# Value columns of a projection in two double blocks: products of 512 columns instead of 256

## The chip, the cores and the metric

The kernel runs on one core of a Trainium2 chip. The metric is the device time of one execution in microseconds, the median of several runs. The core's engines are TensorE (matmuls, PE in the profile, PEld its weight loads), VectorE (DVE), ScalarE (ACT), GpSimd (POOL) and SyncE (SP); 16 DMA engines move data.

## The reference, cut to what matters

One block of a network: a normalized input `xn` (256 tokens, 2048 wide) and a normalized context `cn` (256 tokens) are multiplied by a wide matrix `w_in`, and the columns of the product feed a windowed attention and two gated scans.

```
aq, ak, av, ag, hq, hff, hfb, hi, hg, ma, mb = split_columns(xn @ w_in[l])
caq, cak, cav, cag, chq, chff, chfb, chi, chg, cma, cmb = split_columns(cn @ w_in[l])
...
v_h = to_heads(hi)
cv_h = to_heads(chi)
```

The change touches the columns `hi` and `chi` alone: the 2048 values (from column 11264, `C_HI`) of the scans, for the 256 tokens and the 256 of the context. All is float32.

## The kernel before

`xH` and `xL` (one tile, `xHL`) hold the 512 normalized rows, transposed and split in a high and a low part, so that one float32 product is three matmuls: high by high, low by high and high by low. Weights arrive as raw tiles of 128x1024 (`wload`, 5 buffers, one load of 512 KB on SP's queue). ScalarE rounds a raw tile to its high part `wh`, and VectorE subtracts it to get the low part `wl` (`two`, three buffers each). I call the work of one such pair a chunk.

The stage of the change computes five groups of columns after the output gates: values (4 calls of `quad_tok`), keys and values of the attention (2 calls), and then the forget gates (`quad_col`). They use a scheme with seven products instead of eight for a 2x2 block product: the tokens are halved (latent and context halves side by side), the 2048 rows of K are halved, and the columns of a block are halved. `token_sums` has put sums of token parts in `S`; `combos` makes the combinations of the weight blocks b11, b12, b21, b22 on VectorE; `ORDER` lists the seven products, each with its weight combination and its token operand (a part of `xHL` or of `S`).

`quad_tok(col0, dst)` does 512 columns in two column halves of 256. It loops over two halves `s` of the K rows of a block. In each it loads four raw tiles (one for each weight block, 4 row tiles by 256 columns), and for each of the seven products makes one chunk and issues 24 matmuls of 256 moving columns: 16 with `wh` (L732, L734) and 8 with `wl` (L737). A product has its own bank of the accumulating memory (tiles `pj` and `pm`) through both halves of K. After the second half `done_with` adds the banks up: ScalarE copies out two, and VectorE makes seven additions of 512 columns. Two stores of 512 KB on POOL's queue put the result in `v_dr`. In one call there are 2 x 7 chunks and 336 matmuls; four calls give 56 chunks and 1344 matmuls.

The names in the instructions: `T` is a buffer for a weight combination (two of them, in turn), `vo` a result, `sn` a sum on the way, `sgg` and `hg` belong to the output gates. `tc.high_priority` moves an instruction forward in the order that the scheduler writes for VectorE and ScalarE; TensorE's order is the code's order. Each queue runs its instructions in order.

Of the kernel before, what the change touches and what calls it, by code (L numbers as in the profile page):

```python
# [7 lines left out]
F32 = mybir.dt.float32  # L8
F32R = mybir.dt.float32r
U8 = mybir.dt.uint8  # L10
AF = mybir.ActivationFunctionType
ALU = mybir.AluOpType
PSUM = bass.MemoryType.PSUM

P = 128
# [6 lines left out]
PRIO = 100000  # L22

C_Q, C_K, C_V, C_G = 0, 2048, 2560, 3072
C_HQ, C_FF, C_FB, C_HI, C_HG = 5120, 7168, 9216, 11264, 13312
# [13 lines left out]
def block_kernel(ctx: ExitStack, tc: tile.TileContext, x, c, cx, c_ctx, w_ada, b_ada, norm_gain, w_in,  # L39
                 b_merge, lb_f, lb_b, hg_gain, w_oh, sink, w_oa, w_out, fin_gain, cst, msk, out):  # L40
    nc = tc.nc
    pe, act, dve, pool = nc.tensor, nc.scalar, nc.vector, nc.gpsimd

    def pl(name, bufs=1, **kw):
        return tc.tile_pool(name=name, bufs=bufs, **kw)
# [3 lines left out]
    fp = ctx.enter_context(pl("fp", side="right"))  # L49
    pad = ctx.enter_context(pl("pad"))  # L50
    base = ctx.enter_context(pl("base"))
# [9 lines left out]
    def wload(w, row0, nk, col0, ncol, rp=None):  # L61

        raw = (rp or wp).tile([P, 1024], F32, tag="raw", name="raw", bufs=8 if rp else 5)
        rv = raw[:, : len(col0) * nk * ncol].rearrange("p (g k c) -> p g k c", g=len(col0), k=nk)
        for g, co in enumerate(col0):
            nc.sync.dma_start(rv[:, g], w[row0: row0 + nk * P, co: co + ncol].rearrange("(k p) c -> p k c", p=P))
        return raw, rv
# [37 lines left out]
    def bank(name="pj"):  # L105
        return pj.tile([P, 512], F32, tag="pj", name=name)
# [122 lines left out]
    v_dr = [[dram.tile([P, 1024], F32, name=f"v{g}_{t}") for t in range(2)] for g in range(4)]  # L229
# [275 lines left out]
    def bank8():  # L505

        i = turn8[0] % 8
        turn8[0] += 1
        return bank() if i < 4 else ps.tile([P, 512], F32, tag=("tp", "o", "al1", "al2")[i - 4], name="pm")
# [5 lines left out]
    def pairs_of(a):  # L515
        return a.rearrange("p (a t) -> p a t", a=2)

    def run(g):
        for _ in g:
            pass  # L520
# [3 lines left out]
    def send():  # L524
        while outs:
            o = outs.pop(0)
            nc.scalar.dma_start(*o[:2])
            tasks.extend(o[2:])

    def output_gate(g):  # L530
        bg = yield from proj_tok_g(w_in, C_HG + 512 * g, x_st, range(2))
        for t in range(2):
            sg = base.tile([P, 512], F32, tag="sm", name="sgg", bufs=3)
            act.activation(sg, bg[t], AF.Sigmoid)
            dve.tensor_tensor(sg, bg[t], sg, op=ALU.mult)
            outs.append((hg_dr[g][:, t * 512: (t + 1) * 512], sg))
# [24 lines left out]
    with pl("sp", reuse_waits="tile") as sp:  # L561
# [3 lines left out]
        def tmp():  # L565
            t_at[0] ^= 1
            return sp.tile([P, 1024], F32, tag="T", name="T") if t_at[0] else \
                fp.tile([P, 1024], F32, tag="acc", name="T")
# [33 lines left out]
        def sums(i):  # L602
            return lambda k: S[:, :, i, k, :].rearrange("p z (a t) -> p z a t", a=2)

        def sides(h, kh):
            return lambda k: xHL[:, :, 8 * kh + k, :].rearrange("p z (a h t) -> p z a h t", a=2, h=2)[:, :, :, h, :]

        ORDER = ((0, "b11", sides(0, 0)), (1, "t1", sums(0)), (2, "t2", sums(1)), (3, "b22", sums(3)),
                 (4, "t3", sums(2)), (5, "b21", sides(0, 1)), (6, "t4", sides(1, 1)))

        def combos(b):


            def sub(o, x_, y_):
                with tc.high_priority(PRIO):
                    dve.tensor_tensor(o, x_, y_, op=ALU.subtract)  # L616

            t = tmp()
            yield b["11"]
            sub(t, b["12"], b["11"])  # L620
            yield t
            sub(t, b["22"], t)
            yield t
            yield b["22"]
            sub(b["12"], b["22"], b["12"])
            yield b["12"]
            yield b["21"]
            sub(t, b["21"], t)
            yield t

        def two(src):
            h = wp.tile([P, 1024], F32R, tag="wh", name="wh", bufs=3)
            lo = wp.tile([P, 1024], F32R, tag="wl", name="wl", bufs=3)
            with tc.high_priority(PRIO):
                act.activation(h, src, AF.Copy)  # L635
                dve.tensor_tensor(lo, src, h.bitcast(F32), op=ALU.subtract)  # L636
            return h, lo
# [49 lines left out]
        def quad_tok(col0, dst):  # L687

            m_ = [None] * 7
            out = [fp.tile([P, 2, 512], F32, tag="F0", name="vo", bufs=2) for _ in range(2)]  # L690
            sn = {}

            def add(o, x_, y_):
                dve.tensor_tensor(o, x_, y_, op=ALU.add)

            def done_with(i):


                def place(t, c):
                    return out[t][:, :, c * T: (c + 1) * T]  # L700

                with tc.high_priority(2 * PRIO):
                    if i < 2:
                        sn[i] = base.tile([P, 512], F32, tag="sm", name="sn", bufs=3)
                        act.activation(sn[i], m_[i], AF.Copy)
                    elif i == 2:
                        sn[2] = base.tile([P, 512], F32, tag="bb", name="sn", bufs=2)
                        add(sn[2], m_[2], sn[0])
                    elif i == 3:
                        sn[3] = base.tile([P, 512], F32, tag="bb", name="sn", bufs=2)  # L710
                        add(sn[3], sn[2], sn[1])
                        add(place(0, 1), pairs_of(m_[3]), pairs_of(sn[3]))
                    elif i == 4:
                        add(sn[2], m_[4], sn[2])
                        add(place(1, 1), pairs_of(sn[2]), pairs_of(sn[1]))
                    elif i == 5:
                        add(place(0, 0), pairs_of(m_[5]), pairs_of(sn[0]))
                    else:
                        add(place(1, 0), pairs_of(m_[6]), pairs_of(sn[2]))

            for s in range(2):
                b = {n: wload(w_in, 1024 * (n[0] == "2") + 512 * s, 4, (col0 + T * (n[1] == "2"),), T)[0]
                     for n in ("11", "12", "22", "21")}
                for (i, _, st_), src in zip(ORDER, combos(b)):
                    h, lo = [a.rearrange("p (k c) -> p k c", k=4) for a in two(src)]
                    if s == 0:
                        m_[i] = bank8()
                    st4 = [(k, z) for k in range(4) for z in range(2)]
                    for k, z in st4:
                        o = m_[i][:, z * T: (z + 1) * T]  # L730
                        sh, sl = [st_(4 * s + k)[:, a, z, :] for a in range(2)]
                        pe.matmul(o, sh, h[:, k, :], start=s == 0 and k == 0 and z == 0, stop=False,  # L732
                                  skip_group_check=True)
                        pe.matmul(o, sl, h[:, k, :], start=False, stop=False, skip_group_check=True)  # L734
                    for k, z in st4:
                        o = m_[i][:, z * T: (z + 1) * T]
                        pe.matmul(o, st_(4 * s + k)[:, 0, z, :], lo[:, k, :], start=False,  # L737
                                  stop=s == 1 and k == 3 and z == 1, skip_group_check=True)
                    if s == 1:
                        done_with(i)  # L740
            for t in range(2):
                nc.gpsimd.dma_start(dst[t], out[t].rearrange("p a c -> p (a c)"))

        with tc.manual_schedule(engines={mybir.EngineType.PE}):
            for g in range(3):
                run(output_gate(g))
                send()
                if g < 2:
                    token_sums(g)
            for g in range(4):  # L750
                quad_tok(C_HI + 512 * g, v_dr[g])
            for i, co in enumerate((C_K, C_V)):
                quad_tok(co, kv_dr[i])
            for n in range(1, 8):
                for d in range(2):
                    if (d, n) != (0, 1):
                        quad_col(d, 2 * n)
# [702 lines left out]
    for n in range(3):  # L1460
        bo = [bank() for _ in range(2)]
        for k0 in range(0, KT, 2):
            h, lo = wchunk(w_out, k0 * P, 2, n * 512, 512)
# [8 lines left out]
    for k0 in range(0, KT, 4):  # L1472
        h, lo = wchunk(w_out, k0 * P, 4, D - 512, 256)
# [8 lines left out]
    for t in range(2):  # L1482
# [12 lines left out]
        for c0, c1, on_act in ((0, 512, True), (512, 1024, False), (1024, 1536, True), (1536, D, False)):  # L1495
            o_ = xv[t][:, c0: c1]
# [62 lines left out]
```

## Time and profile before

| | |
|---|---|
| median of 3 runs | 1584.49 us (1583.45 to 1588.19) |
| the profiled execution | 1586.59 us, its span 1584.8 us |
| granted TensorE clock, mean | 0.999 |
| output gates, last chunk begins | 195.5 us |
| values (4 calls of `quad_tok`) | 198.2 to 359.5 us |
| K and V of the attention (2 calls) | 359.5 to 440.1 us |
| forget gates | 440.1 to about 700 us |

Times in the profile are from the start of the span. A row that groups instructions has their count, busy time, mean length in ns, and, behind the bar, the idle time of the engine just ahead of them and what ended it. A matmul's length overlaps that of the next, so the pace of TensorE is read from the distance between starts.

### The profile page before, as it was taken

The numbers are of one execution on the slowest core, as the hardware profiler recorded it, in microseconds if no ns is written. First come the engines' busy times: TensorE is split into PE (matmuls) and PEld (weight loads), VectorE is DVE, ScalarE is ACT, GpSimd is POOL, SyncE is SP. The second block draws the span as 40 slices with busy tenths as digits, with TensorE's granted clock in tenths as the row PEclk, the third lists the DMA queues.
The fourth block names the chain that finished last, engine by engine and source line by source line (L and its number), as shares of the span: only waits on it lengthen the run. The fifth ranks groups of instructions, "written<-read, shape, count | busy, mean of one in ns | idle before, by whom it ended". The sixth has DMA issues, their size and how long they took to land. (4 is left out here: it accounts for less than half of the span.)

```text
span 1584.8 us, 27868 instructions
## 1 busy us (share of the span) xinstructions
PE 1561.6 (99%) x10954; PEld 1343.8 (85%) x10954; DVE 1201.5 (76%) x1764; ACT 860.5 (54%) x1344; POOL 142.1 (9%) x280
## 2 busy tenths in 40 slices
PE   7999999999999999999999999999999999999998
PEld 4568899999988888888888888888888888888887
DVE  4449977777787878878888897888878777757764
ACT  4336443333355555566656666575666776744442
POOL 2000000000000000011212222121121000000000
PEclk9999999999999999999999999999999999999999
DMA  9996734434444444467777877878677854458661
GB/s 366 386 387 230 226 111 130 134 132 134 133 147 127 134 130 137 136 225 252 243 247 244 300 260 233 270 243 273 221 261 249 289 159 154 155 180 295 226 197 69
DMA packets 242900, 333.83 MB, mean 211 GB/s; under 512 B 12080, under 2 KB 162000, under 8 KB 242000
## 3 DMA queue, kind: packets, MB, share of 16 engines
q1 hardware_dynamic: 214096, 249.54, 48.5%
q0 software_dynamic: 19168, 64.08, 11.8%
q10 hardware_dynamic: 9504, 18.42, 3.2%
q8 instruction: 86, 1.41, 0.4%
q14 instruction: 46, 0.38, 0.1%
HBM read 300.53 MB, written 31.47 MB: 209 GB/s over the span
## 5 line engine op out<-in xcount | busy, mean ns | idle before, releaser
L85 ACT ACTIVATE wh<-raw 128x1024 fp32r<-128x1024 f32 x284 | 298.8, 1059 | 236.3 <-PE pj L101 151.7
L86 DVE TENSOR_TENSOR wl<-raw,wh 128x1024 fp32r<-128x1024 f32 x284 | 344.0, 1219 | 89.9 <-ACT wh L85 88.9
L100 PE MATMUL pj<-wh,xHL 128*128 128x512 f32 (+1 forms) x768 | 298.6, 390 | 0.0
L101 PE MATMUL pj<-wh,xHL 128*128 128x512 f32 (+1 forms) x768 | 294.8, 385 | 0.0
L103 PE MATMUL pj<-wl,xHL 128*128 128x512 f32 (+1 forms) x768 | 202.7, 385 | 0.0
L635 ACT ACTIVATE wh<-T 128x1024 fp32r<-128x1024 f32 x75 | 79.5, 1060 | 166.8 <-DVE T L616 83.9
L100 PEld LDWEIGHTS pj<-wh,xHL 128*128 128x128 f32 x768 | 144.4, 188 | 28.2 <-ACT sg L219 0.6
L101 PEld LDWEIGHTS pj<-wh,xHL 128*128 128x128 f32 x768 | 144.5, 188 | 27.6
L103 PEld LDWEIGHTS pj<-wl,xHL 128*128 128x128 f32 x768 | 142.0, 188 | 28.9
L635 ACT ACTIVATE wh<-raw 128x1024 fp32r<-128x1024 f32 x100 | 105.3, 1055 | 71.9 <-PE pj L734 23.7
L154 PE MATMUL pj<-xHL,wh 128*128 128x512 f32 x512 | 130.3, 396 | 0.0
L636 DVE TENSOR_TENSOR wl<-raw,wh 128x1024 fp32r<-128x1024 f32 x100 | 121.8, 1218 | 9.8 <-ACT wh L635 9.7
L636 DVE TENSOR_TENSOR wl<-T,wh 128x1024 fp32r<-128x1024 f32 x75 | 91.5, 1220 | 32.8 <-ACT wh L635 32.8
L154 PEld LDWEIGHTS pj<-xHL,wh 128*128 128x128 f32 x512 | 92.4, 189 | 16.9
L157 PEld LDWEIGHTS pj<-xHL,wl 128*128 128x128 f32 x512 | 69.8, 190 | 5.2
L204 DVE SCALAR_TENSOR_TENSOR acc<-hgw,cg,acc 128x512 f32<-128x512 f32 x60 | 44.9, 748 | 35.0 <-DMA hgw<-in_w_ada_dram 35.0
L157 PE MATMUL pj<-xHL,wl 128*128 128x256 f32 x512 | 71.3, 282 | 0.0
L912 DVE TENSOR_TENSOR A<-A,X 128x512 f32<-128x512 f32 x96 | 61.6, 682 | 0.1
L616 DVE TENSOR_TENSOR T<-raw,T 128x1024 f32<-128x1024 f32 x50 | 60.9, 1218 | 0.1
L616 DVE TENSOR_TENSOR raw<-raw 128x1024 f32<-128x1024 f32 x25 | 30.6, 1225 | 36.7 <-DMA raw<-in_w_in_dram 36.7
L541 POOL DMA_DIRECT2D hgw<-in_w_ada_dram x64 | 35.0, 547 | 235.3 <-DVE acc L204 157.6
L660 PE MATMUL pj<-S,wh 128*128 128x512 f32 x208 | 52.6, 395 | 1.6 <-ACT s L667 1.6
(353 smaller groups left out, 3155.1 us busy)
## 6 DMA issues: line engine op xcount, KB each, us to landing
raw<-in_w_in_dram SPq DMA_DIRECT2D x300, 512.0 KB, 4.6
raw<-in_w_ada_dram SPq DMA_DIRECT2D x64, 512.0 KB, 8.0
hgw<-in_w_ada_dram POOLq DMA_DIRECT2D x64, 256.0 KB, 4.5
raw<-in_w_o_hgrn_dram SPq DMA_DIRECT2D x32, 512.0 KB, 3.6
raw<-in_w_o_attn_dram SPq DMA_DIRECT2D x32, 512.0 KB, 4.1
raw<-in_w_out_dram SPq DMA_DIRECT2D x28, 512.0 KB, 4.1
F<-F POOLq DMA_DIRECT2D x16, 512.0 KB, 7.2
F<-F ACTq DMA_DIRECT2D x13, 512.0 KB, 4.4
```

Source lines behind the costliest of these rows:

```text
L85: last_hi[0] = act.activation(h[:, :n], raw[:, :n], AF.Copy).ins
L86: last_lo[0] = dve.tensor_tensor(lo[:, :n], raw[:, :n], h[:, :n].bitcast(F32), op=ALU.subtract).ins
L100: pe.matmul(o, s[0], m[0], start=first, stop=False)
L101: pe.matmul(o, s[1], m[0], start=False, stop=False)
L103: pe.matmul(o, s[0], m[1], start=False, stop=last)
L154: pe.matmul(o.rearrange("p (a t) -> p a t", a=2), h[:, j, cs_], xHL[:, :, k0 + j, :T], start=k0 + j == 0, stop=False)
L157: pe.matmul(o[:, :T], lo[:, j, cs_], xH[:, k0 + j, :T], start=False, stop=k0 + j == KT - 1)
L616: dve.tensor_tensor(o, x_, y_, op=ALU.subtract)
L635: act.activation(h, src, AF.Copy)
L636: dve.tensor_tensor(lo, src, h.bitcast(F32), op=ALU.subtract)
L660: pe.matmul(m_[z].rearrange("p (z a t) -> p z a t", z=2, a=2), h[:, k, :], mv(k), start=fresh and k == 0, stop=False, skip_group_check=True)
L912: dve.tensor_tensor(av, av, f.unsqueeze(3).to_broadcast([P, 2, n2, b]), op=ALU.mult)
```

## The change

Two calls of a new function, `quad_wide(b)`, take the place of the four calls of `quad_tok` for the values. The attention's K and V and the forget gates stay as they are.

- One call does 1024 columns in two column halves of 512. A raw tile is now 2 row tiles by 512 columns, and a chunk is 12 matmuls of 512 moving columns: 8 with `wh`, 4 with `wl`. Each weight block needs two raw tiles, so that each product is two chunks and a half of K needs 8 raw tiles and 14 chunks. Two calls give again 56 chunks, with 672 matmuls.
- Both `T` buffers together hold one weight combination.
- A product fills two banks, one for each half of the tokens. There are three pairs of banks for each half of K, not seven banks for a call: products 0, 2, 4 and 6 are accumulated in pair 0, products 1 and 3 in pair 1, product 5 has pair 2. What pair 0 and pair 1 hold after products 0, 1 and 2 is copied out by ScalarE (`kept`, in the buffers F0 and F1), and VectorE adds it to a bank after products 3, 4 and 5.
- Each half of K stores its result on its own, in 3 stores of 512 KB and 2 of 256 KB on POOL's queue. The second half's stores add to what stands in memory (`accum_op`), so that the two halves of K meet there.

```
def quad_wide(b):
    def less(o, x_, y_):
        with tc.high_priority(PRIO):
            for o_, a_, b_ in zip(o, x_, y_):
                dve.tensor_tensor(o_, a_, b_, op=ALU.subtract)
    def weights(s):
        def load(n):
            return [wload(w_in, 1024 * (n[0] == "2") + 512 * s + 256 * c, 2,
                          (C_HI + 1024 * b + 512 * (n[1] == "2"),), 512)[0] for c in range(2)]
        u = [tmp(), tmp()]
        b11 = load("11")
        yield b11
        b12 = load("12")
        less(u, b12, b11)
        yield u
        b22 = load("22")
        less(u, b22, u)
        yield u
        yield b22
        less(b12, b22, b12)
        yield b12
        b21 = load("21")
        yield b21
        less(u, b21, u)
        yield u
    for s in range(2):
        m_ = [[bank8(), bank8()] for _ in range(3)]
        into = {0: (0, True), 1: (1, True), 2: (0, False), 3: (1, False), 4: (0, False), 5: (2, True),
                6: (0, False)}
        kept = {}
        def store(o, t, c, z=slice(0, 2)):
            kw = {"accum_op": ALU.add} if s else {}
            nc.gpsimd.dma_start(v_dr[2 * b + c][t].rearrange("p (z c) -> p z c", z=2)[:, z, :], o, **kw)
        def done_with(i, m):
            with tc.high_priority(2 * PRIO):
                if i < 3:
                    kept[i] = fp.tile([P, 2, 512], F32, tag="F1" if i == 2 else "F0", name="part",
                                      bufs=1 if i == 2 else 2)
                    for z in range(2):
                        act.activation(kept[i][:, z, :], m[z], AF.Copy)
                elif i < 6:
                    o = kept[5 - i]
                    for z in range(2):
                        dve.tensor_tensor(o[:, z, :], m[z], o[:, z, :], op=ALU.add)
                    store(o, *((0, 1), (1, 1), (0, 0))[i - 3])
                else:
                    for z in range(2):
                        o = base.tile([P, 512], F32, tag="bb", name="part", bufs=2)
                        act.activation(o, m[z], AF.Copy)
                        store(o, 1, 0, z)
        for (i, _, st_), tiles in zip(ORDER, weights(s)):
            z_, fresh = into[i]
            for c in range(2):
                h, lo = [a.rearrange("p (k c) -> p k c", k=2) for a in two(tiles[c])]
                jz = [(j, z) for j in range(2) for z in range(2)]
                for j, z in jz:
                    for a in range(2):
                        pe.matmul(m_[z_][z], st_(4 * s + 2 * c + j)[:, a, z, :], h[:, j, :],
                                  start=fresh and c == 0 and j == 0 and a == 0, stop=False,
                                  skip_group_check=True)
                for j, z in jz:
                    pe.matmul(m_[z_][z], st_(4 * s + 2 * c + j)[:, 0, z, :], lo[:, j, :], start=False,
                              stop=c == 1 and j == 1, skip_group_check=True)
            done_with(i, m_[z_])
...
-            for g in range(4):
-                quad_tok(C_HI + 512 * g, v_dr[g])
+            for b in range(2):
+                quad_wide(b)
```

The order of instructions is the same on every engine outside this stage. Inside it, VectorE's order before, at the end of the first call of `quad_tok` (`wl_2178` is the last chunk's low part, `wl_2220` that of the next call's first, `T_2218` and `T_2434` combinations for the next call and half):

```order
L636 TENSOR_TENSOR wl_2178<-T_1992,wh_2177 128x1024
L694 TENSOR_TENSOR vo_1766<-pj_1870,sn_2113 128x2x256
L694 TENSOR_TENSOR sn_2083<-pm_1900,sn_2083 128x512
L636 TENSOR_TENSOR wl_2220<-raw_2210,wh_2219 128x1024
L694 TENSOR_TENSOR vo_1767<-sn_2083,sn_2052 128x2x256
L694 TENSOR_TENSOR vo_1766<-pm_1929,sn_2021 128x2x256
L636 TENSOR_TENSOR wl_2250<-T_2218,wh_2249 128x1024
L616 TENSOR_TENSOR T_2434<-raw_2428,raw_2426 128x1024
L616 TENSOR_TENSOR T_2218<-raw_2214,T_2218 128x1024
L694 TENSOR_TENSOR vo_1767<-pm_1959,sn_2083 128x2x256
L636 TENSOR_TENSOR wl_2280<-T_2218,wh_2279 128x1024
```

A combination is made one product ahead, and for the next half already, in the other buffer. VectorE's order now, at the end of the first half of K of the first `quad_wide` (L750 is `less`, L796 an addition of `done_with`; `raw_2054` and `raw_2056` are b11 of the next half, `raw_2093` and `raw_2095` its b12, `raw_2134` and `raw_2136` its b22; `wl_2025` is the last chunk of this half, `wl_2059`, `wl_2075`, `wl_2100` and `wl_2116` are chunks 0 to 3 of the next; `part_1810` is what is kept of product 0):

```order
L750 TENSOR_TENSOR T_2052<-raw_2093,raw_2054 128x1024
L636 TENSOR_TENSOR wl_2025<-T_1773,wh_2024 128x1024
L750 TENSOR_TENSOR raw_2093<-raw_2134,raw_2093 128x1024
L750 TENSOR_TENSOR T_2053<-raw_2095,raw_2056 128x1024
L796 TENSOR_TENSOR part_1810<-pm_1770,part_1810 128x512
L796 TENSOR_TENSOR part_1810<-pm_1771,part_1810 128x512
L636 TENSOR_TENSOR wl_2059<-raw_2054,wh_2058 128x1024
L636 TENSOR_TENSOR wl_2075<-raw_2056,wh_2074 128x1024
L636 TENSOR_TENSOR wl_2100<-T_2052,wh_2099 128x1024
L750 TENSOR_TENSOR T_2052<-raw_2134,T_2052 128x1024
L750 TENSOR_TENSOR raw_2095<-raw_2136,raw_2095 128x1024
L636 TENSOR_TENSOR wl_2116<-T_2053,wh_2115 128x1024
```

Four subtractions for the next half stand among the splits of chunks -1 to 3; `raw_2136` goes into the buffer that `raw_2054` leaves. POOL's order before, for all of the values:

```order
L742 DMA v0_0_107<-vo_1766 128x1024
L742 DMA v0_1_108<-vo_1767 128x1024
L742 DMA v1_0_109<-vo_2208 128x1024
L742 DMA v1_1_110<-vo_2209 128x1024
L742 DMA v2_0_111<-vo_2650 128x1024
L742 DMA v2_1_112<-vo_2651 128x1024
L742 DMA v3_0_113<-vo_3092 128x1024
L742 DMA v3_1_114<-vo_3093 128x1024
```

These are two stores for each call. Now, for the first of two calls (the first five rows are the first half of K, the last five add to the same tiles in memory):

```order
L783 DMA v1_0_109<-part_1892 128x1024
L783 DMA v1_1_110<-part_1851 128x1024
L783 DMA v0_0_107<-part_1810 128x1024
L783 DMA v0_1_108<-part_2040 128x512
L783 DMA v0_1_108<-part_2043 128x512
L783 DMA v1_0_109<-part_2172 128x1024
L783 DMA v1_1_110<-part_2131 128x1024
L783 DMA v0_0_107<-part_2090 128x1024
L783 DMA v0_1_108<-part_2320 128x512
L783 DMA v0_1_108<-part_2323 128x512
```

Ten stores for each call stand where four stood for the same columns.

More of the change, by code (lines that the diff above doesn't have):

```diff
@@ L742, in quad_tok @@
                 nc.gpsimd.dma_start(dst[t], out[t].rearrange("p a c -> p (a c)"))
+        def quad_wide(b):
+            def less(o, x_, y_):
+                with tc.high_priority(PRIO):
+                    for o_, a_, b_ in zip(o, x_, y_):
[20 more added lines that the diff above has]
+                yield u
+            for s in range(2):
+                m_ = [[bank8(), bank8()] for _ in range(3)]
[6 more added lines that the diff above has]
+                def done_with(i, m):
+                    with tc.high_priority(2 * PRIO):
+                        if i < 3:
+                            kept[i] = fp.tile([P, 2, 512], F32, tag="F1" if i == 2 else "F0", name="part",
+                                              bufs=1 if i == 2 else 2)
+                            for z in range(2):
+                                act.activation(kept[i][:, z, :], m[z], AF.Copy)
+                        elif i < 6:
+                            o = kept[5 - i]
+                            for z in range(2):
+                                dve.tensor_tensor(o[:, z, :], m[z], o[:, z, :], op=ALU.add)
+                            store(o, *((0, 1), (1, 1), (0, 0))[i - 3])
+                        else:
+                            for z in range(2):
+                                o = base.tile([P, 512], F32, tag="bb", name="part", bufs=2)
[3 more added lines that the diff above has]
+                    z_, fresh = into[i]
+                    for c in range(2):
+                        h, lo = [a.rearrange("p (k c) -> p k c", k=2) for a in two(tiles[c])]
[4 more added lines that the diff above has]
+                                          start=fresh and c == 0 and j == 0 and a == 0, stop=False,
+                                          skip_group_check=True)
+                        for j, z in jz:
+                            pe.matmul(m_[z_][z], st_(4 * s + 2 * c + j)[:, 0, z, :], lo[:, j, :], start=False,
+                                      stop=c == 1 and j == 1, skip_group_check=True)
+                    done_with(i, m_[z_])
@@ L749, in block_kernel @@
                     token_sums(g)
-            for g in range(4):
-                quad_tok(C_HI + 512 * g, v_dr[g])
+            for b in range(2):
+                quad_wide(b)
             for i, co in enumerate((C_K, C_V)):
```

## The prediction

> **What bounds the kernel now.** I read the page first, then the table by stage, then TensorE's order of time, then who waits for whom in the stage that changes. The page (busy time; granted clock and traffic in 40 slices):
>
> ```profile
> span 1584.8 us, 27868 instructions
> ...
> PE 1561.6 (99%) x10954; PEld 1343.8 (85%) x10954; DVE 1201.5 (76%) x1764; ACT 860.5 (54%) x1344; POOL 142.1 (9%) x280
> ...
> PEclk9999999999999999999999999999999999999999
> ...
> GB/s 366 386 387 230 226 111 130 134 132 134 133 147 127 134 130 137 136 225 252 243 247 244 300 260 233 270 243 273 221 261 249 289 159 154 155 180 295 226 197 69
> ```
>
> TensorE is busy for 99% of the span at a full clock. The table by stage (values, then K and V by the same function, then the forget gates):
>
> ```profile
> core 0: us, PE busy (x) PEld busy (x) DVE busy (x) ACT busy (x) POOL busy (x), PEclk, DMA share, GB/s
> 198.20:359.50 161.30, 161.30 (x1346) 161.28 (x1345) 119.97 (x118) 63.08 (x66) 3.73 (x7) 1.00 0.40 130
> 359.50:440.10 80.60, 80.60 (x674) 80.60 (x673) 60.06 (x58) 31.15 (x32) 2.13 (x4) 1.00 0.41 131
> 440.10:700.00 259.90, 257.59 (x1468) 225.97 (x1467) 206.95 (x233) 150.68 (x194) 5.75 (x14) 1.00 0.46 138
> ```
>
> The values take 161.3 us in which TensorE never stops, while VectorE has 26% left, ScalarE 61% and the DMA engines 60%. So the stage lasts as long as its matmuls, and what counts is how far apart they start. TensorE in order of time (start, length, instruction; the last matmuls of the output gates, two chunks of the values, the first of K):
>
> ```profile
> 192.77 0.39 PE L100 MATMUL pj<-wh,xHL 128*128 128x512 f32 x1
> 195.49 0.39 PE L100 MATMUL pj<-wh,xHL 128*128 128x512 f32 x1
> 198.21 0.28 PE L732 MATMUL pj<-wh,xHL 128*128 128x256 f32 x1
> ...
> 241.40 0.28 PE L732 MATMUL pj<-wh,S 128*128 128x256 f32 x1
> 244.28 0.28 PE L732 MATMUL pj<-wh,S 128*128 128x256 f32 x1
> ...
> 359.48 0.28 PE L732 MATMUL pm<-wh,xHL 128*128 128x256 f32 x1
> ```
>
> Each of these rows begins a chunk of weights (1024 columns of raw tile). A chunk of the values is 24 matmuls of 256 columns in 2.88 us, 120.0 ns each; 359.48 - 198.21 = 161.27 is 56 such chunks without a gap. A chunk of the output gates is 12 matmuls of 512 columns in 2.72 us, 226.7 ns each. Two narrow ones (240.0) cost 13.3 ns more than one wide one.
>
> **The change part by part.** *Matmuls.* 1344 of 256 columns become 672 of 512; the columns streamed and the 56 chunks stay. Each chunk then has the form of the output gates' (12 matmuls, contiguous wide moving operand, pairs into alternate banks), so 2.72 us: 56 x 0.16 = 8.96 us less. The stationary operands are those of now, xHL halves and S, and both kinds run at the same 120.0 ns now. The other wide products, in the forget gates, bound it from the other side:
>
> ```profile
> 471.02 2.00 PE L660 MATMUL pm<-S,wh 128*128 128x512 f32 x8
> 472.87 1.11 PE L663 MATMUL pm<-S,wl 128*128 128x256 f32 x8
> ```
>
> There 8 take 1.85 us, 231 ns each, with a moving operand read in pieces; at that rate a chunk is 2.77 us and the gain 56 x 0.11 = 6.0 us. I take 2.72, whose form is the new one's. The Trainium skill (TensorE: Matmul & The Clock Gate, Back-to-back issue gap) gives N/2.4 + 2.5 ns, 109.2 and 215.8, so a gain of 672 x 2.6 = 1.7 us as an estimate; both rows here are about 11 ns above it, and the trace disagrees.
>
> *VectorE and ScalarE.* Groups of the values' stage (count, busy, mean):
>
> ```profile
> L636 DVE TENSOR_TENSOR wl<-raw,wh 128x1024 fp32r<-128x1024 f32 x32 | 39.0, 1219 | 4.2 <-ACT wh L635 4.1
> L636 DVE TENSOR_TENSOR wl<-T,wh 128x1024 fp32r<-128x1024 f32 x24 | 29.3, 1221 | 14.7 <-ACT wh L635 14.7
> L616 DVE TENSOR_TENSOR T<-raw,T 128x1024 f32<-128x1024 f32 x16 | 19.5, 1219 | 0.0
> L694 DVE TENSOR_TENSOR vo<-pj,sn 128x512 f32<-128x512 f32 x6 | 4.1, 685 | 0.9 <-PE pj L737 0.9
> L635 ACT ACTIVATE wh<-raw 128x1024 fp32r<-128x1024 f32 x32 | 33.6, 1055 | 29.8 <-PE pj L734 20.1 <-PE pm L734 6.6 <-ACT sn L705 2.2
> L705 ACT ACTIVATE sn<-pm 128x512 f32<-128x512 f32 x5 | 2.9, 579 | 0.0
> ```
>
> The 56 splits and 32 subtractions stay. VectorE's adds go from 28 to 24 (-2.7 us at 0.685), ScalarE's copies out of the banks from 8 to 32 (+13.9 us at 0.579). That makes VectorE about 117 of 152 us (77%) and ScalarE 77 of 152 (51%): both hidden under TensorE, but in order, so the question is whether one instruction stands behind a late one.
>
> *Banks.* Bank pair 0 takes products 0, 2, 4 and 6, so ScalarE must copy it out between them: product 2 begins 5.44 us after product 0 ends, and the two copies need 1.2 us behind at most one split of 1.06. No cost; the 5.44 us of the product between is the cover.
>
> *Loads and the order on VectorE.* Both halves of a weight block must now be there, so 8 raw tiles pass through the 5 buffers per half of K, and both T buffers serve one half. VectorE in order of time near the end of a quad_tok, with a wait for a load in brackets:
>
> ```profile
> 228.79 1.22 DVE L616 TENSOR_TENSOR raw<-raw 128x1024 f32<-128x1024 f32 x1 [2.88 <-DMA raw<-in_w_in_dram]
> 229.94 0.68 DVE L694 TENSOR_TENSOR sn<-pj,sn 128x512 f32<-128x512 f32 x1
> 230.54 1.21 DVE L636 TENSOR_TENSOR wl<-raw,wh 128x1024 fp32r<-128x1024 f32 x1
> ```
>
> Times from issue to landing of this stage's loads and stores (median last), and of the output gates' loads, which have the wide rows:
>
> ```profile
> raw<-in_w_in_dram SPq DMA_DIRECT2D x32, 512.0 KB, 3.5
> v<-vo POOLq DMA_DIRECT2D x7, 512.0 KB, 2.9
> ```
> ```profile
> raw<-in_w_in_dram SPq DMA_DIRECT2D x16, 512.0 KB, 4.4
> ```
> ```profile
> DMA to landing us min/median/max: 3.3/3.5/5.1
> ```
>
> The last row is the spread of the first.
>
> A 1024-column step occupies VectorE for 1.15 us and a 512-column one for 0.60. I follow the new order at the end of a half, with 0 where TensorE begins the next half's chunk 0, and a split of chunk c not before chunk c-3 ends, at 2.72 (c-2), since wl has three buffers. The adds of product 5 (`part_1810`) end at -2.73, the split of chunk 0 (`wl_2059`) at -1.58; only that frees the buffer of the tile `raw_2136`, which lands 3.5 later, at 1.92. VectorE splits chunk 1 and, from 0, chunk 2, subtracts once, and at 2.30 comes to `raw_2095<-raw_2136`, already landed (at 4.4 to landing it waits 0.5). The split of chunk 3 behind it ends at 4.60; TensorE wants it at 8.16 + 8 x 0.227 = 9.97. So the tile may take 3.5 + 0.38 + 5.37 = 9.25 us to land before TensorE waits, against 5.1 for the slowest load of this stage. Behind it in SP's queue stands `raw_2247`, whose first reader comes three steps later. I put these waits at 0, with 0 to 4 us for the range.
>
> *Stores.* POOL issues 20 instead of 8, of about 0.53 us each, with nothing behind them but each other; 4 MB more is written, and half the stores (second halves of K) add in memory. The trace has no adding store. It should lie between a plain store, 2.9 us to landing, and a load followed by a store, 3.5 + 2.9 = 6.4 (2.2 times). The copies into the F0 buffers need them back 14.4 us (buffer of product 1) and 12.3 us (of product 0) after the adds: hidden at both ends. I take no cost for them; what they may do to the loads is a rival below. The values are read much later than they are stored:
>
> ```profile
> L1059 POOL DMA_DIRECT2D v<-v x32: 538/539/548, 693.1 to 1173.5; - x32
> ```
>
> *Everything else.* Outside this stage the order on every engine is unchanged, so K and what follows move up as a block.
>
> Sum: the profiled execution took 1586.59 us (span 1584.8), 2.1 above the median of the runs, 1584.49. 1586.59 - 8.96 = 1577.6 for it; against the median, 1575.5.
>
> **The rivals.**
> *The adding stores hold up the loads: slower.* Around the boundary at the end of a second half, 1 MB of adding stores is issued between -2.7 and +1.5, together with the load of `raw_2136`. At 387 GB/s, the most the page shows, 1 MB holds all DMA engines for 2.7 us; at k times a plain store's work, 2.7k. If all of it goes ahead of the load, TensorE waits 2.7k - 5.75, at two boundaries. At k = 2.2 that is 0.4 for both; the gain is gone at k = 3.8, and k = 5 gives 1584.5 - 9.0 + 15.5 = 1591. For it: the 2.2 comes from times to landing, and no row shows how long an add holds an engine. Against it: the engines serve the queues by turns, as the 0.40 share with loads landing in 3.5 to 5.1 beside stores suggests.
>
> *Waits take half the gain.* The forget gates have VectorE at 80% and ScalarE at 58%, near what this stage will have, and TensorE idles 2.3 of 259.9 us there. With that at the 4 half boundaries and a late tile or two, 4 to 8 us come back: 1580 to 1584, no change that can be told. Against it: the margin of 5.4 us above.
>
> *The fixed cost does not halve.* If a wide matmul ran at 237 ns here, the chunk would be 2.85 us and the gain 1.7: 1582.8. Against it: no wide row quoted is above 231. The Trainium skill's rule (TensorE: Matmul & The Clock Gate) gives the same time.
>
> **How the numbers follow.** A change within 0.3% (4.75 us) is about what a measurement of this kernel cannot tell. The forecast (gain 6 to 10, 1574.5 to 1578.5) gets 0.70; waits that take half 0.13; a fixed cost that does not halve 0.04; slow adding stores 0.12, of which 0.02 ends within 0.3%; a gain of more than 10 us 0.01. So faster 0.71, same 0.19, slower 0.10. I predict 1575.5; the range, 1573.5 to 1583, keeps the first three cases.
>
> **What would show it.** TensorE: wide rows of the new stage 227 ns apart, K's first matmul near 350.5 instead of 359.5, no idle of TensorE between. VectorE near 77%, ScalarE near 51% there. Adding stores landing in 3 to 7 us, raw tiles still in 3.5 to 5. The forecast is wrong if TensorE waits for wl or wh at the half boundaries, above all behind second halves of K, or if the wide matmuls start more than 231 ns apart.

## The result, and the profile after

The changed kernel takes 1577.99 us (median of 6 runs, 1575.88 to 1580.47); the kernel before, run beside it, 1585.80 us (1583.45 to 1588.19). The ratio is 0.9951, 95% interval 0.9938 to 0.9965: 7.8 us less. The profiled execution took 1578.92 us. Its page:

```profile
span 1577.1 us, 26598 instructions
...
PE 1553.2 (98%) x10282; PEld 1309.2 (83%) x10282; DVE 1200.7 (76%) x1760; ACT 874.2 (55%) x1368; POOL 152.3 (10%) x292
```

672 matmuls fewer, and 8.4 us less of TensorE. The table by stage, for the values (second row: K and V, which are as before):

```profile
core 0: us, PE busy (x) PEld busy (x) DVE busy (x) ACT busy (x) POOL busy (x), PEclk, DMA share, GB/s
199.77:352.07 152.30, 152.30 (x673) 126.17 (x672) 120.18 (x115) 74.38 (x89) 12.47 (x18) 1.00 0.55 162
352.07:432.70 80.63, 80.63 (x673) 80.60 (x672) 58.74 (x58) 32.24 (x34) 3.38 (x5) 1.00 0.47 137
```

TensorE still has no idle time in the stage, but the stage is 9.0 us shorter. Its weight loads now take 83% of the time and not 100%. The price is on the DMA engines, whose share went from 0.40 to 0.55. TensorE in order of time (the first chunks, the last, and K's first matmul; a row holds several matmuls):

```profile
199.77 1.98 PE L811 MATMUL pj<-wh,xHL 128*128 128x512 f32 x8
201.59 1.07 PE L815 MATMUL pj<-wl,xHL 128*128 128x512 f32 x4
202.49 1.98 PE L811 MATMUL pj<-wh,xHL 128*128 128x512 f32 x8
...
349.37 1.98 PE L811 MATMUL pj<-wh,xHL 128*128 128x512 f32 x8
351.19 1.07 PE L815 MATMUL pj<-wl,xHL 128*128 128x512 f32 x4
352.09 0.28 PE L732 MATMUL pj<-wh,xHL 128*128 128x256 f32 x1
```

From 199.77 to 352.09 is 152.32 us, 56 chunks of 2.72, and 202.49 - 199.77 is one of them. The stage begins 1.56 us later than in the trace of before, with an unchanged order ahead of it. VectorE in order of time at the second boundary between halves of K (199.77 + 28 x 2.72 = 275.93, the end of the first second half, so with adding stores around it), and then times to landing of the stage's loads and stores:

```profile
276.32 1.23 DVE L636 TENSOR_TENSOR wl<-T,wh 128x1024 fp32r<-128x1024 f32 x1 [0.74 <-ACT wh L635]
277.58 1.23 DVE L750 TENSOR_TENSOR T<-raw,T 128x1024 f32<-128x1024 f32 x1
279.93 1.23 DVE L750 TENSOR_TENSOR raw<-raw 128x1024 f32<-128x1024 f32 x1 [1.13 <-DMA raw<-in_w_in_dram]
281.08 1.22 DVE L636 TENSOR_TENSOR wl<-T,wh 128x1024 fp32r<-128x1024 f32 x1
```
```profile
raw<-in_w_in_dram SPq DMA_DIRECT2D x32, 512.0 KB, 4.0
v<-part POOLq DMA_DIRECT2D x12, 512.0 KB, 4.1
v<-part POOLq DMA_DIRECT2D x6, 256.0 KB, 4.9
```
```profile
DMA to landing us min/median/max: 3.3/4.0/6.6
DMA to landing us min/median/max: 2.8/4.9/8.1
```

The first row of the last fence is of the raw tiles, the second of the 18 stores issued inside the stage (of 20; two follow). Loads land later than before (4.0 against 3.5; at most 6.6 against 5.1), most of all at the boundaries, and VectorE waits there: the tile that the subtraction `raw<-raw` reads was issued 1.46 us ahead of the boundary and took 5.4 us to land, so that VectorE comes to it 4.00 us behind the boundary. The split of chunk 3 behind it ends at 282.30, 6.37 us behind the boundary; TensorE wants it at 9.97.

### The profile page after: what moved, and what is told of

Its sections match the earlier page's. It is cut to its first block, busy times and chain, and to the rows that moved or that the text cites. A ratio compares the mean times of both kernels' runs of the same rounds, so it can differ in the third digit from the quotient of the medians.

```text
span 1577.1 us, 26598 instructions
## 1 busy us (share of the span) xinstructions
PE 1553.2 (98%) x10282; PEld 1309.2 (83%) x10282; DVE 1200.7 (76%) x1760; ACT 874.2 (55%) x1368; POOL 152.3 (10%) x292
## 4 chain that ended last, share of the span: by engine, by line
PE 93%; DMA 3%; DVE 2%; SPq 1%; issue 1%; ACT 0%; POOLq 0%; POOL 0%; DVEq 0%; ACTq 0%
PE pj L100 12%; PE pj L101 12%; PE pj L103 12%; PE pj L154 7%; PE pm L660 5%; PE pj L660 4%; PE pj L157 4%; PE pj L811 3%; PE pm L811 3%; PE pm L663 2%; PE pj L663 2%; PE pj L427 2%; PE pj L815 2%; PE pm L815 2%; PE pa L323 2%; PE al L941 1%
## 5 line engine op out<-in xcount | busy, mean ns | idle before, releaser
L660 PE MATMUL pm<-S,wh 128*128 128x512 f32 x208 | 52.7, 395 | 0.7 <-ACT s L667 0.7
L100 PE MATMUL pj<-wh,bH 128*128 128x512 f32 x128 | 50.2, 392 | 0.0
```

Of the source, the lines that this page charges most:

```text
L100: pe.matmul(o, s[0], m[0], start=first, stop=False)
L660: pe.matmul(m_[z].rearrange("p (z a t) -> p z a t", z=2, a=2), h[:, k, :], mv(k), start=fresh and k == 0, stop=False, skip_group_check=True)
```

## Experiments

Each variant was timed beside the kernel before, on the same chip; ratios are to that kernel.

**The changed kernel once more.**

> The changed kernel once more, as the yardstick for the other runs on this chip. Every theory expects a ratio to the kernel before of 0.994 to 0.9965 (0.995 so far) and a values stage of 56 x 2.72 = 152.3 us with no idle time of TensorE. The profiled execution of the changed kernel began the stage 1.56 us later than the one before, though the order of instructions ahead of the stage is the same: if that is variation between executions, the stage begins anywhere from 198 to 200 us here; if it belongs to the change, it begins near 199.8 again.

Measured: 1579.94 us, ratio 0.9956 (0.9939 to 0.9973). The stage lasts 152.30 us and begins at 198.15, so the 1.56 us of the other trace is variation between executions. Raw tiles took up to 8.0 us here (the tile behind the one just named, which is read later), and TensorE still did not wait in the stage.

**The pace of the matmuls alone.** The high-part products (the low-part ones likewise):

```
-  pe.matmul(m_[z_][z], st_(...)[:, a, z, :], h[:, j, :], ...)
+  for e in (slice(0, 256), slice(256, 512)):
+      pe.matmul(m_[z_][z][:, e], st_(...)[:, a, z, :], h[:, j, e], ...)
```

> The changed kernel with each matmul of 512 columns cut into two of 256 with the same stationary operand: 1344 matmuls again, all else (banks, copies, adds, loads, stores) as changed. Theory (the whole gain is the pace of the matmuls, 2 x 120.0 ns against 226.7): chunks of 2.88 us, the stage 161.3 us again, the time within 0.2% of the kernel before (ratio 0.999 to 1.001), 8.9 us above the changed kernel. Rival (part of the gain came from another side, fewer adds on VectorE, other banks, loads with longer rows): the ratio stays below 0.998. Rival (the changed loads and stores cost TensorE something that the faster matmuls paid for): the ratio is above 1.002.

Measured: 1585.90 us (11 runs), ratio 0.9990 (0.9981 to 1.0000). The table by stage, for the values:

```profile
197.80:359.10 161.30, 161.30 (x1345) 161.26 (x1344) 120.67 (x115) 74.34 (x89) 12.47 (x18) 1.00 0.55 156
```

With narrow matmuls and everything else as changed, the stage has the old 161.3 us, the old 100% of weight loads, and the new 0.55 of the DMA engines. So the 9.0 us of the stage are the pace of the matmuls, and the other parts of the change neither gave nor took time there. The 0.1% by which this variant stays below 1 is at the edge of its interval; nothing in its trace accounts for it.

**What a matmul costs beside its columns.** The same with cuts at 320 instead of 256:

> The changed kernel with each matmul of 512 columns cut into 320 and 192 with the same stationary operand. Theory A (each matmul costs its columns plus a fixed 13.3 ns, since 512 columns take 226.7 ns and 256 take 120.0, so 0.4167 ns a column): a pair takes 213.3 + 26.6 = 240 ns, as two of 256 do, a chunk 2.88 us, the stage 161.3 us, the time as with halves of 256. Theory B (what costs the time is the next weight load, which keeps its engine 100% busy beside matmuls of 256 columns and 83% beside 512: no matmul is shorter than one load, about 111 to 120 ns): 192 columns take 111 to 120 ns instead of 93, 320 take 147, a pair 258 to 267, a chunk 3.10 to 3.20, the stage 174 to 179 us, so 21 to 27 us more than the changed kernel. The distance between the starts of the matmuls decides.

Measured: 1599.53 us (2 runs), ratio 1.0081 (1.0054 to 1.0109). The stage and, in order of time, weight loads (PEld) from inside it, then matmuls of the same stretch (a row can hold several; its form is that of the first):

```profile
199.75:373.54 173.79, 173.79 (x1346) 173.79 (x1344) 121.03 (x115) 74.36 (x89) 12.47 (x18) 1.00 0.51 145
```
```profile
230.00 0.19 PEld L817 LDWEIGHTS pj<-wl,S 128*128 128x128 f32 x1
230.15 0.19 PEld L817 LDWEIGHTS pj<-wl,S 128*128 128x128 f32 x1
230.26 0.19 PEld L817 LDWEIGHTS pj<-wl,S 128*128 128x128 f32 x1
```
```profile
229.98 0.42 PE L817 MATMUL pj<-wl,S 128*128 128x320 f32 x2
230.15 0.42 PE L817 MATMUL pj<-wl,S 128*128 128x192 f32 x2
230.23 0.34 PE L817 MATMUL pj<-wl,S 128*128 128x320 f32 x1
```

A chunk is 173.79 / 56 = 3.10 us, a pair 258.6 ns: theory B's total, and 18.6 ns more than theory A's 240, while the weight loads are busy all the time (173.79 us of 173.79). How a pair is shared out is not shown. The loads start 0.15 and 0.11 us apart in turn, which fits 147 ns for 320 columns and a floor of about 111 for the 192, whose columns and 13.3 ns would make 93. But the matmuls themselves start 0.17 us behind one of 320 and 0.08 behind one of 192. So 0.4167 ns a column and 13.3 ns fit 256 and 512 columns and miss this pair; that a weight load of 128x128 sets a floor for each matmul is theory B's reading, and stays one. The forecast needed only the price at 256 and 512. The Trainium skill (TensorE: Matmul & The Clock Gate, Back-to-back issue gap) says that in a real stream the spacing is set by the weight load and the matmul together, and gives 81 ns for 128 columns and 131 for 512: the pair agrees with the rule, but 512 columns took 226.7 ns here, and the 81 was not tested.

**K and V in the same way**, one call more of `quad_wide`:

```
-  for i, co in enumerate((C_K, C_V)):
-      quad_tok(co, kv_dr[i])
+  quad_wide(C_K, kv_dr)
```

> The changed kernel with the attention's K and V columns (2 calls of quad_tok, 28 chunks of narrow matmuls) done in one call of quad_wide too. Theory (a chunk is 2.72 instead of 2.88 us and everything else is hidden): 28 x 0.16 = 4.5 us less than the changed kernel, K and V in 76.2 instead of 80.6 us, ratio to the kernel before about 0.992. Rival (what follows, the forget gates with VectorE at 80%, sits behind a half boundary with adding stores and loses it again): ratio 0.994 to 0.995, with new idle time of TensorE behind the stage.

Measured: 1575.15 us, ratio 0.9928 (0.9913 to 0.9943), 4.8 us below the changed kernel on the same chip, where 4.5 were forecast. Values, then K and V:

```profile
197.70:350.00 152.30, 152.30 (x673) 126.11 (x673) 120.26 (x115) 75.07 (x89) 12.44 (x18) 1.00 0.56 162
350.00:426.20 76.20, 76.20 (x337) 63.09 (x337) 59.34 (x56) 36.87 (x45) 7.09 (x10) 1.00 0.62 169
```

TensorE has no idle time in either stage, and in the forget gates behind them it waits 2.2 us in all for ScalarE, as before (2.3), so the rival's new idle time did not come. This version is the fastest of all.

**Plain stores.** `kw = {}` for both halves of K:

> The changed kernel with plain stores for the second half of K: the sum of the two halves of K of the values is left out, nothing else. Theory (adding is hidden): the time of the changed kernel within 0.1%, stage 152.3 us, no idle time of TensorE; only the landing of the stores (4 to 5 us to about 3), POOL's issue (0.9 to 0.53 us) and the DMA engines' share (0.55 to about 0.45) come down, and the loads land in 3.5 instead of 4.0 us. Rival (adding holds up the loads and costs TensorE a little somewhere): 1 to 3 us less than the changed kernel.

Measured: 1581.16 us, ratio 0.9952 (0.9938 to 0.9967), the changed kernel's within the interval. The stage lasts 152.3 us here too, so the adding costs no time in it. It does cost the DMA engines: the queue of the stores in the stage (packets, MB, share of all 16 engines over 153 us), in the changed kernel and here:

```profile
q0 software_dynamic: 2219, 7.45, 20.1%
```
```profile
q0 software_dynamic: 2208, 7.87, 14.0%
```

Plain: 0.140 x 153 / 7.87 = 2.72 us of all engines for a MB. In the changed kernel 4.19 of the 7.45 MB are plain (11.4 us), and the other 3.26 MB take 30.8 - 11.4 = 19.4 us, 5.9 for each: 2.2 times a plain store. The loads' median did not fall as expected (4.2 us), and the engines' share fell to 0.51 only, not to 0.45. But the last two tiles issued ahead of the second boundary landed in 4.4 and 5.2 us, where the changed kernel has 5.4 and 6.6, and 5.6 and 8.0 in its other trace: there the adding does delay the loads.

**Twice the stores**, each issued a second time to spare memory:

```
-  nc.gpsimd.dma_start(v_dr[2 * b + c][t]..., o, **kw)
+  for dst in (v_dr[2 * b + c][t], *[x[2 * b + c][t] for x in v_more]):
+      nc.gpsimd.dma_start(dst..., o, **kw)
```

> The changed kernel with every store of the stage issued twice, the second to spare memory of its own, adding where the first adds: 40 stores on POOL's queue instead of 20, 8.4 MB more written, 4 of it in adding stores issued close to the half boundaries. Theory (the stores are hidden, with room): the DMA engines' share goes from about 0.55 to about 0.78 (the stores' queue holds 20% of the engines' time now), TensorE waits 0 to 3 us in the stage, ratio to before 0.995 to 0.9975. Rival (slow adding stores hold up the tile that is wanted at a half boundary; 2 MB of them at 2 x 2.7 us each would be 10.8 - 5.75 = 5 us at each of two boundaries): TensorE waits about 10 us for a load or wl, ratio 1.000 to 1.003.

Measured: 1600.03 us, ratio 1.0075 (1.0046 to 1.0105): by the ratios about 20 us above the changed kernel, more than even the rival forecast. The idle times of TensorE in order of time, with what ended them:

```profile
277.68 1.19 PE L818 MATMUL pm<-wl,xHL 128*128 128x512 f32 x4 [2.02 <-DVE wl L638]
319.66 2.03 PE L818 MATMUL pj<-wl,xHL 128*128 128x512 f32 x4 [1.95 <-DVE wl L638]
375.39 2.08 PE L739 MATMUL pj<-wl,S 128*128 128x256 f32 x8 [9.89 <-DVE wl L638]
```

VectorE had waited for a raw tile each time:

```profile
272.94 1.23 DVE L752 TENSOR_TENSOR raw<-raw 128x1024 f32<-128x1024 f32 x1 [5.33 <-DMA raw<-in_w_in_dram]
314.91 1.23 DVE L752 TENSOR_TENSOR raw<-raw 128x1024 f32<-128x1024 f32 x1 [5.26 <-DMA raw<-in_w_in_dram]
372.97 1.23 DVE L618 TENSOR_TENSOR T<-raw 128x1024 f32<-128x1024 f32 x1 [15.10 <-DMA raw<-in_w_in_dram]
```

The first is at a boundary behind adding stores, but not at the subtraction that the forecast followed: it is the one ahead of it (`raw_2093<-raw_2134` in the order shown with the change), whose tile was issued between the adding stores of products 3 and 4 and took 11.1 us. The split of chunk 0 stands behind it. The second is at the boundary after a first half, where the stores just ahead are plain. The longest stands in K, behind the last adding stores. Raw tiles issued from 330 to 350 us, the store queue in the stage, and the DMA engines while K begins (columns of the table by stage):

```profile
DMA to landing us min/median/max: 3.7/5.5/22.5
```
```profile
q0 software_dynamic: 3976, 13.21, 32.4%
```
```profile
355.00:367.00 12.00, 10.50 (x77) 9.83 (x75) 2.50 (x3) 4.51 (x6) 4.48 (x6) 1.00 1.06 226
```

By the times of their packets all engines are busy (1.06; packets overlap, so the share can pass 1), and yet they move only 226 GB/s. With 8.39 MB plain at 2.72 us, the other 4.82 MB of the queue take 5.6 us each, against 5.9 above. TensorE's waits add up to 13.9 us; most of the rest is the granted clock (PEclk, third from the end) behind each of them:

```profile
277.00:279.00 2.00, 1.32 (x5) 1.14 (x6) 2.00 (x3) 1.06 (x1) 2.00 (x5) 0.94 0.62 47
279.00:281.00 2.00, 2.00 (x6) 1.53 (x5) 1.97 (x2) 0.00 (x0) 2.00 (x4) 0.50 0.91 172
281.00:283.00 2.00, 2.00 (x7) 1.58 (x7) 0.16 (x1) 0.64 (x1) 1.09 (x2) 0.70 0.93 258
283.00:285.00 2.00, 2.00 (x10) 1.65 (x10) 0.98 (x1) 1.39 (x3) 0.00 (x0) 1.00 1.07 244
```

Here two microseconds of idle time are followed by 3.4 at half the clock. The Trainium skill (TensorE: Matmul & The Clock Gate, Why this matters for your kernels) warns of gaps above about 3 us; here 1.95 and 2.02 us were enough. Length alone does not decide it, as the next kernel shows.

**Four times the stores**, the same with three spare copies:

> The same with every store issued four times: 80 stores, 25 MB more. By the queue's share (20% of 152 us for the 20 stores, 34% for the loads) loads and stores would want about 190 us of all the DMA engines in a stage of 152. Theory (the hidden transfers become the bound when they no longer fit): TensorE waits some 5 to 40 us in the stage, the most if nothing of the stores can be left over for the next stage, ratio to before 0.998 to 1.02, the DMA engines' share near 1. Rival (the stores fall back behind the loads and drain during K and V, where 0.6 of the engines' time is free): no more than 3 us, ratio below 0.998.

Measured: 1610.71 us (2 runs), ratio 1.0152 (1.0113 to 1.0191). TensorE waits 23 us, among them for something new (us in total, times, longest), and the DMA engines' share in the values is 0.90:

```profile
PE pm L814 <- ACT part L795: 7.5, 2, 4.6
PE pj L739 <- DVE wl L638: 6.7, 1, 6.7
PE pm L739 <- DVE wl L638: 5.2, 1, 5.2
```

The copies into F0 (`part`, L795) now wait for the buffers that the stores hold, and TensorE for the bank. The stores do not simply fall back behind the loads. One of these waits, longer than the 2 us above, left the clock at 1.00:

```profile
288.55 2.14 PE L814 MATMUL pm<-wh,S 128*128 128x512 f32 x8 [2.88 <-ACT part L795]
```
```profile
289.00:291.00 2.00, 1.69 (x8) 1.05 (x6) 2.00 (x2) 1.93 (x2) 0.00 (x0) 1.00 1.03 244
```

**Twice the stores, all plain:**

> Every store of the stage issued twice as in the doubled kernel before it, but all 40 as plain stores: the sum of the two halves of K of the values is left out. The doubled adding stores cost about 20 us (TensorE idle 9.9, 2.0 and 1.9 us for wl behind late raw tiles, and a granted clock of 0.50 for some microseconds behind each idle time). Theory (it is the adding: all the DMA engines are held 5.5 to 5.8 us for each MB added, 2.7 for each MB stored plainly, and the loads wait their turn behind it): 53 us of loads and 46 us of stores fit, raw tiles land in at most 7 us, TensorE waits less than 1 us, ratio 0.995 to 0.997. Rival (it is the number of stores or their bytes, not the adding): idle time behind late raw tiles stays, ratio above 1.000.

Measured: 1580.83 us, ratio 0.9967 (0.9949 to 0.9985). Store queue, and landing of the raw tiles in the stage:

```profile
q0 software_dynamic: 4403, 15.73, 28.2%
```
```profile
DMA to landing us min/median/max: 3.4/4.3/7.1
```

Twice the MB at the plain price (2.74 us a MB), tiles within 7.1 us, no idle time in the stage, not at the boundaries behind first halves either. So it takes the adding to cost 20 us, not the number of stores; how it reached the second wait, behind plain stores, stays open.

**Twice the stores of the values, K and V by `quad_wide`:**

> The kernel with the attention's K and V done by quad_wide too, with every store of the values (not of K and V) issued twice, the second halves adding in both places. In the doubled kernel the longest idle time of TensorE (9.9 us) came at the start of K, whose raw tiles have rows of 1 KB and took 15 to 22 us to land behind 2 MB of adding stores, while the tiles with rows of 2 KB took up to 11.6 us. Here K's tiles have rows of 2 KB. Theory (the engines take the queues by turns, one row at a time, so a tile of short rows gets half the share): tiles at the start of K land in at most 12 us, idle time there 0 to 3 us, ratio to before 0.994 to 1.000. Rival (the loads go behind the adding stores whatever their rows): tiles take 15 us or more there too, idle time near 10 us, ratio 1.002 to 1.006.

Measured: 1590.67 us (10 runs), ratio 1.0028 (1.0013 to 1.0044). Tiles issued from 330 to 350 us, and TensorE's longest idle time:

```profile
DMA to landing us min/median/max: 3.6/5.0/16.1
```
```profile
367.93 2.08 PE L818 MATMUL pj<-wl,xHL 128*128 128x512 f32 x4 [7.13 <-DVE wl L638]
```

16.1 us against 22.5, 7.1 of idle time against 9.9: less, but the theory's bounds (12 us, 3 us) are missed, and the ratio is the rival's. The order of VectorE's work at the start of K changed with the rows, so even the part that became less is not shown to be theirs; what shares out the engines between the two queues stays open.

**The kernel before once more, and TensorE's instructions moved.**

> The kernel before once more, for a second trace of it. The forecast counted every stage but the values as unchanged; the profiled executions of the changed kernel and of its variants show 0.8 to 2.6 us of idle time of TensorE at one of the al matmuls behind 900 us, which the one trace of before doesn't show. If that belongs to executions and not to the change, this trace has it too, or has idle time of that size elsewhere; its stage of the values lasts 161.3 us and begins between 197 and 200 us.

> The changed kernel with the 12 matmuls of the first of the 56 chunks in each half of K cut into two of 256 columns: 48 matmuls and 48 weight loads more in TensorE's instructions, 0.64 us (48 x 13.3 ns) more in the stage, nothing else. In the kernels with 672 wide matmuls TensorE idles 1.4 to 2.7 us, waiting for nothing that the profile shows, ahead of the last of 128 short al matmuls near 1215 us, at the same instruction each time; where the stage has 1344 matmuls it idles 0.7 to 0.9 us near 1023 us, or not at all. Theory (instructions arrive in pieces of 16.4 KB, 256 instructions of 64 bytes by estimate from the traffic of the instruction queue; 128 al matmuls and their weight loads are 256 in 1.1 us, and where a piece ends just behind them two pieces are wanted too close together): 96 instructions more put the end of a piece in the middle of the run, so the idle time at that instruction is gone or under 0.5 us, and what comes instead is under 1 us. Rival (TensorE waits there for something else, such as a bank or the clock): the same 1.4 to 2.7 us at the same instruction. The time is the changed kernel's within 0.15% either way.

The edit of the second cuts `if i == 0 and c == 0`. Measured: 1585.83 us for the one run of before (values, K and V 241.9 us together, as in the first trace); 1579.70 us, ratio 0.9950 (0.9933 to 0.9968), for the shifted kernel. The idle times for which the profile names no cause, in order of the changed kernel, its other trace, the kernel before (second trace) and the shifted one:

```profile
1214.69 0.22 PE L941 MATMUL al<-so,acc 128*32 128x64 f32 x1 [1.41 <-issue]
```
```profile
1215.50 0.22 PE L941 MATMUL al<-so,acc 128*32 128x64 f32 x1 [2.61 <-issue]
```
```profile
1022.76 0.31 PE L866 MATMUL al<-so,acc 128*32 128x64 f32 x6 [0.71 <-issue]
```
```profile
1016.14 0.54 PE L943 MATMUL al<-so,acc 128*32 128x64 f32 x24 [0.42 <-issue]
```

All six traces with 672 wide matmuls and K and V as before idle at the same last matmul of the same run: 1.41, 2.61, 1.62 with plain stores, 1.79 with doubled plain ones, 2.72 and 2.15 with stores issued twice and four times. With K and V by `quad_wide` too, one trace idles 1.64 us at a matmul of an earlier run, at 1011.71, and the other not at all. 96 more instructions far ahead took the wait at 1215 us away and left 0.42 us elsewhere. The time did not show it: 0.9950 against 0.9951 and 0.9956.

Two counts from the traces bear the theory out. Counted from 0 through TensorE's matmuls, weight loads and sequencer instructions, the held-up matmul has the number 14785 (kernel before, halves, 320 and 192), 17089 (the six), 13505 (shifted) or 12738 (K and V too); divided by 256, each leaves 193 or 194. And in each of these eleven traces a packet of 16.4 KB of the instruction queue begins 2.2 to 2.4 us ahead of that matmul. So it hangs on TensorE's instructions coming in pieces of 256, and not on data; why a piece comes too late just there stays open.

## Why the prediction was right, and where it was off

Faster was forecast, 1575.5 us in 1573.5 to 1583; 1577.99 was measured.

- **Matmuls.** The term of 8.96 us (2.72 a chunk) measured 161.27 - 152.32 = 8.95. Taking the price from the output gates, whose form it is, and not from the forget gates, was right; the variant with halves shows that it is the whole gain of the stage.
- **VectorE and ScalarE.** 79% and 49% measured, 77% and 51% forecast; hidden. The copies out of the banks cost TensorE nothing.
- **Loads and the order on VectorE.** No wait of TensorE, as said, but by a smaller margin. The step had the subtraction at 2.30 and the end of the split of chunk 3 at 4.60; it was 4.00 and 6.37. It left out 0.39 us from a late `wh` (276.32 - 275.93) and had the tile land in 3.5 us, where it took 5.4 and VectorE waited 1.13 for it. Nor does 5.1 us, the slowest load of before, bound the new ones: 6.6 and 8.0 were seen, of the tile behind it. The working's own limit of 9.25 us was not reached. 3.6 us were left, not 5.4.
- **Stores.** POOL's issues took 0.69 us on average (12.47 us for 18), not 0.53: plain ones 0.53 to 0.56, as forecast, adding ones 0.86 to 1.22. Adding stores landed in 5.0 to 8.1 us, where 3 to 7 were forecast. An adding store was taken as 2.2 times a plain one, from times to landing; by the times of packets on the engines it is 2.2 (5.9 against 2.72 us a MB), with 2.0 from the doubled run. That the two agree is partly luck, since a time to landing and a time on the engines are different quantities.
- **Slow adding stores.** The mechanism of this rival is real and decides at twice the adding, though one subtraction earlier than forecast and, worst, behind the last half, where K's tiles stand: places that the working did not look at. By its own formula k = 2.2 gave 0.4 us of waits; none came, but twice the stores bring 2 us at two boundaries and 10 at the start of K. The change stands nearer to that point than the 0.12 suggests.
- **A fixed cost that does not halve, and waits that take half,** are ruled out by the 2.72 us and the absence of idle time.
- **Everything else unchanged.** The order is, but not every wait: 1344 instructions fewer on TensorE moved an idle time of 0.7 us or none to a place where it is 1.4 to 2.7. What that takes of the 9.0 us is not settled. From the end of K and V to the end of the span, before took 1584.8 - 440.1 = 1144.7 us and the changed kernel 1577.1 - 432.7 = 1144.4, in spite of its 1.41: other waits were shorter, and this trace falls short of 9.0 because its stage begins 1.56 us later. The other trace took 1580.2 - 431.1 = 1149.1; there the 2.61 us and half the clock behind them stand for most of the difference. The ratio's 7.8 us, with an interval from 5.5 to 9.8, cannot tell the two cases apart.
- **The 2.5 us between 1577.99 and 1575.5:** 1.3 are the yardstick (before is 1585.80 over 6 runs, 1584.49 over the 3 shown), 1.2 a gain that did not arrive, if it is not noise.

## What to carry to other kernels

Where a stage is bound by TensorE, price a matmul by the distance between starts in a stage of the same form, and measure again where the length differs: 320 and 192 columns cost 18.6 ns a pair more than the rule from 256 and 512. An adding store is not a store: count its engine time at twice, and look for the load that is wanted just behind it, because the time between fits and stalls is short. A wait of TensorE of about 2 us can cost more than its length, since the clock can fall behind it.

## What was not expected of the hardware

- By the times of their packets, adding stores hold all 16 DMA engines 5.6 to 5.9 us for a MB (plain 2.72), and a load of 512 KB among doubled ones took up to 22.5 us to land.
- The granted clock can fall to 0.50 for 3.4 us behind 1.95 us of idle time, and behind the 2.61 us at 1215.50 it fell; behind the 1.41 us at 1214.69, and behind 2.88 us with four times the stores, it stayed at 1.00. So the length of the wait is not all that counts.

```profile
1217.00:1219.00 2.00, 2.00 (x6) 1.52 (x6) 0.17 (x1) 1.69 (x6) 0.58 (x2) 0.50 0.76 214
```

- 128 short matmuls in a row can outrun TensorE's supply of instructions by 0.4 to 2.7 us, at one place in every 256 instructions (193 or 194 in these counts); so it depends on how many instructions stand ahead of them.
